# An encoder layer on one core: PSUM laid out by stage with two shared doubles, the output projection in two blocks of 384, and w_in loads moved in the queue

## The chip, the cores and the metric

The kernel runs on one core of a Trainium2 chip. The metric is the device time of one execution in microseconds (us); times are given as the median of several runs. The engines are TensorE (PE, matmuls; PEld are its weight loads), VectorE (DVE), ScalarE (ACT), GpSimd (POOL) and SyncE (SP, which here only issues DMAs). Each has its own instruction stream and works through it in order; they wait for each other by semaphores. PE writes its products into PSUM, a memory of eight banks of 2 KB per partition, from which DVE and ACT read. Everything else works in SBUF.

## What is computed

One layer of an encoder over 512 prompt tokens and 256 sample tokens (two sequences with the same weights), model width 1024, all in fp32:

```
x = layer_norm(ALPHA * x + 0.5 * swiglu(x, ffn1_up, ffn1_down), ln1_g, ln1_b)
u = x @ w_in
u_a, u_b, gate_a, gate_b = split(u)
h_a = rwkv7_branch(u_a, ...) @ w_branch_a        # bidirectional state scan, 8 heads of 64
h_b = retention_branch(u_b, pos) @ w_branch_b    # 4 heads of 128
mix = (sigmoid(gate_a) * h_a + sigmoid(gate_b) * h_b) @ w_out
x = layer_norm(ALPHA * x + mix, ln2_g, ln2_b)
x = layer_norm(ALPHA * x + 0.5 * swiglu(x, ffn2_up, ffn2_down), ln3_g, ln3_b)
```

## The kernel before, in words

Activations lie feature-major: eight tiles of 128 features by 768 tokens (T), of which columns 0 to 511 are the prompt and 512 to 767 the sample (SEGS). fp32 products are made from three fp32r products: `split` (L189 to L191) writes a high part (a cast on ACT) and a low part (a subtraction on DVE), and `mm3` (L202 ff.) sums high by high, high by low and low by high; all these matmuls carry L201. `wtile` (L152 to L163) loads a weight tile on SP's queue (`wr`, L160) and splits it (`wh` L161, `wl` L162).

The stages follow each other: the first feed-forward network (0 to about 530 us, products of 128x384 by a scheme of Strassen's kind, on the halves of the 768 tokens); its layer norm and two lead projections; the preparation (about 576 to 1027 us), in which `prep` and `invert` make the operands of the RWKV scan while `ret_seq` (L640 ff.) computes retention as a filler; the scan (1016 to 1316 us), whose PE order is written by hand (`manual_schedule`), with the gate projections as filler; the merge (`w_b`, `w_a`, then `w_out` with the second layer norm); the second feed-forward network (1507 to 2013 us) and the third layer norm. Outside the hand-written part a scheduler orders each engine's instructions, and it places an instruction by when buffers are expected to come free; so a change of buffers changes the order.

**PSUM.** A double is a tile of 768 fp32 columns in two banks (tag `mm`); a single bank has tag `pc`. `mmps` (L92 to L96) hands out doubles in turn: one lies in a pool `pre` that lives from the start to the scan, the others in the stage's own pool (`psum`, L81). A double can be handed out again when its last reader is done. Before, the first network, the preparation and retention share one pool: `pre` and one more double, and four single banks. The scan has `pre`, four single banks and two for `w`. Merge and second network share a pool of two doubles and four single banks. `small` (L101 to L108, matmuls at L105) uses two single banks, one for each segment. Score tiles of retention (L670, read by the multiplication L673) take a double; its outputs (L679) a single bank; the variance of its norm a double, read last by `osq` (L236).

**Queue around the first network's end.** The last down-projection weights (`in_f1d`, issued at L325) and the first tiles of `w_in` (L160, and L610 for retention's values) are both issued on SP. The `w_in` tiles take buffers of a pool that opens only when the network's are given up, so the issue waits for those.

**Merge.** `merge` loads the retention output (`yb`, tile `t`, L1131) head by head into two buffers (TQ), splits each into `yh` and `yl` (`pair`, L1134 ff.), and multiplies by `w_b` with the gate (`gated`). `finish` closes the last two feature blocks of the RWKV branch (`fin`). `out` (L1151 ff.) multiplies by `w_out` in blocks of columns, BLK[2], and `layer_norm` follows block by block; KEEPO says how many of the eight weight tiles are kept in SBUF from block to block (`reuse`, L177). MPE and VPE say for each block whether sums over features go through PE (1) or are first added up on DVE (0).

Of the kernel before, what the change touches and what calls it, by code (L numbers as in the profile page):

```python
# [8 lines left out]
F32 = mybir.dt.float32  # L9
# [6 lines left out]
PSUM = bass.MemoryType.PSUM  # L16
DRAM = bass.MemoryType.DRAM

P = 128
# [3 lines left out]
T = TP + TS  # L23
SEGS = ((0, TP), (TP, T))
HALVES = ((0, 256), (256, 512), (512, T))
BLK = {1: SEGS, 2: HALVES, 3: SEGS}
FF = 2816
NF = FF // P
W = 512
# [18 lines left out]
FILLS = (2, 1, 2, 1, 1, 1)  # L48
TAIL = ()
EARLY = ('A03', 'B10', 'B11', 'B12', 'B13', 'D03')  # L50
MPE = {1: (0, 1), 2: (0, 0, 0), 3: (0, 1)}
VPE = {1: (1, 1), 2: (0, 0, 1), 3: (1, 1)}
KEEP = 4
CHUNKS = (6, 6, 5, 5)
TH = T // 2
LEAD = 4
RAWS = 10
AHEAD = 9
KEEPO = 1
TQ = 2  # L60
FIN = {0: 1, 1: 1, 2: 1, 3: 1}

# [6 lines left out]
class Builder:  # L69
# [8 lines left out]
        self.n += 1  # L78
        return f"{s}{self.n}"

    def psum(self, ctx, pre=None, **bufs):  # L81
        self.pre, self.turn = pre, 2
        self.pb = bufs
        self.ps = ctx.enter_context(self.tc.tile_pool(name=self.nm("ps"), bufs=1, space=PSUM))

# [4 lines left out]
        return (pool or self.bp).tile([P, T], F32, tag=tag, name=self.nm(s))  # L90

    def mmps(self):  # L92
        self.turn += 1
        if self.pre and self.turn % (self.pb["mm"] + 1) == 0:
            return self.pre.tile([P, T], F32, tag="mm", name=self.nm("mm"))
        return self.ps.tile([P, T], F32, tag="mm", name=self.nm("mm"), bufs=self.pb["mm"])  # L96

    def bank(self, tag="pc"):
        return self.ps.tile([P, 512], F32, tag=tag, name=self.nm(tag), bufs=self.pb[tag])
# [49 lines left out]
    def vcol(self, i):  # L149
        return self.vec[:, i:i + 1]  # L150

    def wtile(self, src, dims, keep=None):  # L152
        nc = self.nc
        n = dims[0] * dims[1]
        self.tiles += keep is None
        raw = self.wp.tile([P, self.wn], F32, tag="wr", name=self.nm("wr"))[:, :n]
        pool, w = (keep, n) if keep else (self.wp, self.wn)
        hi = pool.tile([P, w], F32R, tag="wh", name=self.nm("wh"))[:, :n]
        lo = pool.tile([P, w], F32R, tag="wl", name=self.nm("wl"))[:, :n]
        nc.sync.dma_start(raw.rearrange("p (a b) -> p a b", b=dims[1]), src)  # L160
        nc.scalar.copy(hi, raw)  # L161
        nc.vector.tensor_tensor(out=lo, in0=raw, in1=hi.bitcast(F32), op=ALU.subtract)  # L162
        return tuple(t.rearrange("p (a b) -> p a b", b=dims[1]) for t in (hi, lo))  # L163

    def wparts(self, src, dims, parts):
        n = dims[0] * dims[1]
        raw = self.wp.tile([P, self.wn], F32, tag="wr", name=self.nm("wr"))[:, :n]
        hi = self.wp.tile([P, self.wn], F32R, tag="wh", name=self.nm("wh"))[:, :n]
        lo = self.wp.tile([P, self.wn], F32R, tag="wl", name=self.nm("wl"))[:, :n]
        self.nc.sync.dma_start(raw.rearrange("p (a b) -> p a b", b=dims[1]), src)  # L170
        yield tuple(t.rearrange("p (a b) -> p a b", b=dims[1]) for t in (hi, lo))
        m = n // parts
        for q in range(parts):
            self.split(*(t[:, q * m:q * m + m] for t in (raw, hi, lo)))
            yield
# [127 lines left out]
    def ffn(self, ctx, z, xs, idx, up, down, after, lead, first, then=None):  # L303
# [16 lines left out]
        def raw(src):  # L320
            out = []
            for a in range(0, src.shape[1], m):
                part = src[:, a:min(a + m, src.shape[1])]
                t = fw.tile([P, m * P], F32, tag="wr", name=self.nm("wr"), bufs=RAWS)[:, :part.shape[1] * P]
                nc.sync.dma_start(t.rearrange("p (a b) -> p a b", b=P), part)  # L325
                out.append(t)
            return out

# [268 lines left out]
    def ret_values(self, hp):  # L597
        nc, I, rp = self.nc, self.I, self.rp
        vh = rp.tile([P, 6, 256], F32R, tag="vh", name=self.nm("vh"))
        vl = rp.tile([P, 6, 256], F32R, tag="vl", name=self.nm("vl"))  # L600
        pv = []
        ws = []
        for kh in range(2):
            i = 22 + 2 * hp
            src = I["w_in"][i:i + 2, :, 4 * kh:4 * kh + 4].rearrange("w p k c -> p w k c")
            raw = self.wp.tile([P, 2, 4, P], F32, tag="wr", name=self.nm("wr"))
            wh = self.wp.tile([P, 2, 4, P], F32R, tag="wh", name=self.nm("wh"))
            wl = self.wp.tile([P, 2, 4, P], F32R, tag="wl", name=self.nm("wl"))
            for w in range(2):
                nc.sync.dma_start(raw[:, w], src[:, w])  # L610
            self.split(raw, wh, wl)
            ws.append((wh, wl))
        for tt in range(6):
            if tt % 3 == 0:
                pv.append(self.mmps())
            dst = pv[tt // 3][:, (tt % 3) * 256:(tt % 3) * 256 + 256]
            ts = slice(tt * P, tt * P + P)
            for k in range(KT):
                xh, xl = self.xs[k]
                wh, wl = ws[k // 4]  # L620
                for q, (x, w) in enumerate(((xh, wh), (xh, wl), (xl, wh))):
                    nc.tensor.matmul(dst, x[:, ts], w[:, :, k % 4], start=(k == 0 and q == 0),  # L622
                                     stop=(k == KT - 1 and q == 2))
            if tt % 3 < 2:
                continue
            g = tt // 3
            v = self.b3("v", self.rb)
            nc.scalar.copy(v, pv[g])
            mu = rp.tile([P, 6, 1], F32, tag="mu", name=self.nm("mu"))
            v3 = v.rearrange("p (a e) -> p a e", e=P)  # L630
            nc.vector.tensor_reduce(out=mu, in_=v3, op=ALU.add, axis=AX.X)
            nc.vector.tensor_scalar(mu, mu, 1.0 / P, None, ALU.mult)
            nc.vector.tensor_tensor(out=v3, in0=v3, in1=mu.to_broadcast([P, 6, P]), op=ALU.subtract)
            sl = slice(3 * g, 3 * g + 3)
            self.split(v.rearrange("p (a e) -> p a e", e=256), vh[:, sl], vl[:, sl])
        self.rv = (vh, vl)
        yield
# [232 lines left out]
                yield  # L870

    def segbanks(self):
        ps = self.pre.tile([P, T], F32, tag="mm", name=self.nm("mm"))
        return {(a, b): ps[:, a:b] for a, b in SEGS}

    def scan(self, gates, gd, gp, gt):
# [240 lines left out]
    def merge(self, zp, tp, yb, gd):  # L1117
        nc, I = self.nc, self.I
        with ExitStack() as ctx:
            tq = self.pool(ctx, "tq", TQ)  # L1120
            kp = self.pool(ctx, "kp", KEEPO)
            mp = self.pool(ctx, "mp", 8, "right")
            cy = ctx.enter_context(ExitStack())
            yq = self.pool(cy, "yq", 4)
# [57 lines left out]
                    self.split(m, h[:, a:b], l[:, a:b])  # L1182
                nc.gpsimd.dma_start(z[n], self.x1d[:, n])
            cy.close()
            kept = {}
            self.xs = [self.xpair() for _ in range(KT)]
            for i, seg in enumerate(BLK[2]):
                self.layer_norm(tp, z, 2, self.xs, seg, out(i), halves=True)
# [2 lines left out]
    def build(self, stages=9):  # L1191
# [5 lines left out]
        with ExitStack() as cx:  # L1197
            self.xp = self.pool(cx, "xp", 8)
            ca = cx.enter_context(ExitStack())
            cz = cx.enter_context(ExitStack())  # L1200
            cm = cx.enter_context(ExitStack())
            pre = ca.enter_context(self.tc.tile_pool(name="pre", bufs=1, space=PSUM))
            with ExitStack() as cw:
                self.psum(cw, pre, mm=1, pc=4)
                with ExitStack() as ctx:
                    self.first(ctx)
                self.weights(cm, D)
                cg = ca.enter_context(ExitStack())
                gt = self.pool(cg, "gt", 1, "right")
                with ExitStack() as ctx:  # L1210
                    self.ip = self.pool(ctx, "ip", 1, "right")
                    self.pp = self.pool(ctx, "pp", 1)
                    self.ret_pools(ctx)
                    seq = self.ret_seq(yb)
                    self.prep(lambda i=None: [next(seq, 0) is None for _ in range(1 if i is None else FILLS[i])][-1])
            with ExitStack() as ctx:
                gp = self.pool(ctx, "gp", 1, "right")
                self.gq = self.pool(ctx, "gq", 3)
                self.sp = [self.pool(ctx, "sp", NG // 2) for _ in range(2)]
                self.psum(ctx, pre, pc=4, w=2)  # L1220
                self.S = {}
                with self.tc.manual_schedule(engines={mybir.EngineType.PE}):
                    self.scan([*self.early, *range(AG, KT)], gd, gp, gt)
            ca.close()
            zp = self.pool(cz, "zp", 8, "right")
            self.psum(cx, mm=2, pc=4)
            with ExitStack() as ctx:
                lp = self.pool(ctx, "lp", 1, "right"), ("ln", "acc"), (4, 2)
                z = self.merge(zp, lp, yb, gd)
            cm.close()  # L1230
            for k in range(KT):
                self.dump("x2", z[k], lambda d: d[:, k])
            self.ffn(cx, z, self.xs, 3, I["f2u"], I["f2d"],
                     lambda seg, mean, lp: self.layer_norm(lp, z, 3, None, seg, mean, O["y"]),
                     LEAD, lambda load, ext, tmp: self.forms(z, self.xs, ext, tmp))
# [109 lines left out]
```

## Time and profile before

| what | value |
|---|---|
| time, median of 3 runs | 2044.17 us (2041.85 to 2051.94) |
| the profiled execution | 2045.81 us, span 2044.0 us |
| mean granted clock of TensorE | 0.965 |
| DMA | 202.62 MB, mean 99 GB/s |

The span is the time between the first and the last record of the profile. In rows of groups and chains stand the start, the length in us, the engine, the tile, the line and the count. A row of waits names who waited, for whom, the total, how often, and the longest. "SPq" and "ACTq" are the engines' own instruction queues, mostly issues of DMAs.

### The profile page before, as it was taken

The page shows a single profiled execution, that of the slowest core. Times are in us where ns is not written, and L with a number is a line of the kernel's source. Part 1 is how long each engine was busy: PE and PEld are TensorE (multiplying, and loading weights), DVE is VectorE, ACT ScalarE, POOL GpSimd, SP SyncE. Part 2 cuts the span into 40 slices and gives each one's busy share as a digit, 9 for nine tenths or more (in the row PEclk, how much of TensorE's full clock was granted, in tenths as well). Part 3 has the DMA queues.
Part 4 walks back from the last instruction along what each step waited for, and adds up shares of the span by engine and source line. Part 5 has one row for each costly group of instructions (what it writes and reads, how often), then busy time and mean ns, then how long its engine had stood idle before and what let it go on. Part 6 is the DMA issues. An engine that isn't in the chain of part 4 may idle for free.

```text
span 2044.0 us, 33681 instructions
## 1 busy us (share of the span) xinstructions
PE 1899.9 (93%) x13294; PEld 1696.7 (83%) x13294; DVE 1274.9 (62%) x2265; ACT 827.5 (40%) x1560; POOL 187.2 (9%) x290
## 2 busy tenths in 40 slices
PE   7999999998989889998799989799889999999997
PEld 7999989997777768777688767579879999899985
DVE  8846747565637584857435555377888467475665
ACT  6323323233545353634245555243663224233325
POOL 0000000000000445254420000000000000000000
PEclk9999999998899999999999989999989999999998
DMA  5222121223222333332364441546322221212221
GB/s 196 81 70 73 57 84 59 70 65 98 76 92 96 125 110 106 113 121 102 112 202 113 125 128 62 167 145 212 110 97 85 70 73 58 83 60 64 71 70 64
DMA packets 141598, 202.62 MB, mean 99 GB/s; under 512 B 55680, under 2 KB 73728, under 8 KB 141440
## 3 DMA queue, kind: packets, MB, share of 16 engines
q1 hardware_dynamic: 123904, 178.44, 27.5%
q0 software_dynamic: 3424, 14.94, 2.2%
q10 hardware_dynamic: 14112, 7.08, 1.2%
q8 instruction: 105, 1.72, 0.3%
q14 instruction: 53, 0.43, 0.1%
HBM read 158.74 MB, written 41.68 MB: 98 GB/s over the span
## 4 chain that ended last, share of the span: by engine, by line
PE 80%; DVE 9%; ACT 6%; DMA 3%; issue 2%; ACTq 0%; SPq 0%; DVEq 0%; POOLq 0%
PE mm L201 39%; PE pc L201 29%; PE mm L622 2%; PE pc L246 2%; PE pc L105 1%; PE pc L1038 1%; PE w L974 1%; ACT z L275 1%; DVE wl L162 1%; PE w L985 1%; PE pc L1086 1%; PE w L979 1%; DMA t<-ybd 1%; DVE u L402 1%; DVE z L274 1%
## 5 line engine op out<-in xcount | busy, mean ns | idle before, releaser
L201 PE MATMUL pc<-xh,ph 128*128 128x384 f32 x704 | 243.5, 346 | 20.8 <-ACT u L359 9.2
L201 PE MATMUL pc<-xl,ph 128*128 128x384 f32 x704 | 239.3, 340 | 0.1
L190 ACT CAST ph<-wr 128x512 fp32r<-128x512 f32 (+1 forms) x232 | 131.1, 567 | 220.4 <-PE mm L201 137.4
L201 PE MATMUL mm<-xh,wh 128*128 128x256 f32 (+1 forms) x640 | 181.3, 366 | 27.6 <-DVE s L673 6.1
L402 DVE TENSOR_TENSOR u<-u,pc 128x384 f32<-128x384 f32 x220 | 121.5, 552 | 88.8 <-PE pc L201 85.2
L201 PE MATMUL pc<-eh,ph 128*128 128x384 f32 x528 | 176.4, 334 | 0.0
L201 PE MATMUL pc<-el,ph 128*128 128x384 f32 x528 | 176.4, 334 | 0.0
L201 PE MATMUL mm<-xl,wh 128*128 128x512 f32 (+1 forms) x640 | 173.7, 354 | 0.0
L162 DVE TENSOR_TENSOR wl<-wr,wh 128x1024 fp32r<-128x1024 f32 (+1 forms) x76 | 83.7, 1101 | 138.0 <-PE mm L201 82.4
L201 PEld LDWEIGHTS pc<-xh,ph 128*128 128x128 f32 x704 | 134.8, 192 | 29.8 <-ACT u L359 10.3
L191 DVE TENSOR_TENSOR pl<-wr,ph 128x512 fp32r<-128x512 f32 (+1 forms) x232 | 141.5, 621 | 25.6 <-ACT ph L190 19.9
L201 PE MATMUL pc<-xh,pl 128*128 128x384 f32 x704 | 153.0, 338 | 0.8 <-DVE pl L191 0.8
L191 DVE TENSOR_TENSOR pl<-sa,ph 128x512 fp32r<-128x512 f32 x176 | 120.9, 687 | 45.6 <-ACT ph L190 45.6
L201 PEld LDWEIGHTS mm<-xh,wh 128*128 128x128 f32 x640 | 105.6, 202 | 51.5 <-issue 18.4
L201 PE MATMUL mm<-hl,ph 128*128 128x512 f32 (+1 forms) x544 | 138.8, 336 | 0.0
L201 PE MATMUL mm<-hh,ph 128*128 128x512 f32 (+1 forms) x544 | 138.8, 336 | 0.0
L201 PEld LDWEIGHTS pc<-xl,ph 128*128 128x128 f32 x704 | 134.9, 192 | 0.7 <-DVE xl L191 0.5
L161 ACT CAST wh<-wr 128x1024 fp32r<-128x1024 f32 (+1 forms) x76 | 71.2, 936 | 157.3 <-PE mm L201 130.4
L201 PEld LDWEIGHTS pc<-xh,pl 128*128 128x128 f32 x704 | 126.5, 191 | 1.3 <-DVE pl L191 1.2
L190 ACT CAST ph<-sa 128x512 fp32r<-128x512 f32 x176 | 105.4, 617 | 54.8 <-DVE sa L351 26.3
L201 PE MATMUL mm<-xh,wl 128*128 128x512 f32 (+1 forms) x640 | 125.4, 346 | 0.0
L201 PEld LDWEIGHTS mm<-xl,wh 128*128 128x128 f32 x640 | 104.3, 200 | 15.9
(313 smaller groups left out, 3967.2 us busy)
## 6 DMA issues: line engine op xcount, KB each, us to landing
wr<-in_f1u SPq DMA_DIRECT2D x96, 256.0 KB, 3.2
wr<-in_f2u SPq DMA_DIRECT2D x96, 256.0 KB, 3.1
wr<-in_w_in SPq DMA_DIRECT2D x30, 512.0 KB, 3.5
wr<-in_f1d SPq DMA_DIRECT2D x37, 256.0 KB, 2.7
wr<-in_f2d SPq DMA_DIRECT2D x37, 256.0 KB, 2.7
wr<-in_w_out SPq DMA_DIRECT2D x18, 512.0 KB, 3.5
wr<-in_w_in SPq DMA_DIRECT2D x32, 256.0 KB, 3.5
dd<-ar SPq DMA_DIRECT2D x8, 768.0 KB, 3.3
```

Source lines behind the costliest of these rows:

```text
L105: self.nc.tensor.matmul(ps, w, x[:, a:b], start=True, stop=True)
L161: nc.scalar.copy(hi, raw)
L162: nc.vector.tensor_tensor(out=lo, in0=raw, in1=hi.bitcast(F32), op=ALU.subtract)
L190: self.nc.scalar.copy(hi, src)
L191: self.nc.vector.tensor_tensor(out=lo, in0=src, in1=hi.bitcast(F32), op=ALU.subtract)
L201: self.latest = self.nc.tensor.matmul(o, w, x[:, a:b], start=start and i == 0, stop=stop and i == len(terms) - 1, skip_group_check=more).ins
L246: self.summed = nc.tensor.matmul(st["ps"], self.ones, src, start=k == 0, stop=k == KT - 1).ins
L274: nc.vector.scalar_tensor_tensor(out=zk, in0=zk, scalar=-0.5, in1=rs, op0=ALU.mult, op1=ALU.mult)
L275: nc.scalar.activation(zk, zk, AF.Identity, bias=self.vcol(g0 + 8 + k), scale=self.vcol(g0 + k))
L402: add = lambda o, a, b: nc.vector.tensor_tensor(out=o, in0=a, in1=b, op=ALU.add)
L622: nc.tensor.matmul(dst, x[:, ts], w[:, :, k % 4], start=(k == 0 and q == 0), stop=(k == KT - 1 and q == 2))
L974: nc.tensor.matmul(pb[64 * h:64 * h + 64, C * j:C * j + C], sc[:, c % 4, h, 1], vu[:, c % 4, h], start=True, stop=True)
```

## The change

PSUM: `pre` becomes a tuple of shared doubles. The first network now gets two shared doubles and four single banks; the preparation and retention get these two, one more of their own (three in turn), and two single banks. The scan has the first of the two, four single banks and two for `w`, as before. The merge gets two shared doubles and one of its own and two single banks; the second network the two and four single banks.

Output projection and second normalisation: two blocks, columns 0 to 383 and 384 to 767, where there were three of 256; sums of the first block's squares on DVE and of the second's on PE. Four weight tiles of `w_out` are kept where one was, so there are 10 loads and splits in place of 18, and the pool for them is opened behind the one of the retention output's split.

Queue: `fetch` makes the first six DMA issues of `w_in` follow the last weight load of the first network.

```diff
-BLK = {1: SEGS, 2: HALVES, 3: SEGS}
+BLK = {1: SEGS, 2: ((0, T // 2), (T // 2, T)), 3: SEGS}
...
-MPE = {1: (0, 1), 2: (0, 0, 0), 3: (0, 1)}
-VPE = {1: (1, 1), 2: (0, 0, 1), 3: (1, 1)}
+MPE = {1: (0, 1), 2: (0, 0), 3: (0, 1)}
+VPE = {1: (1, 1), 2: (0, 1), 3: (1, 1)}
...
-KEEPO = 1
+GATED = 6
+KEEPO = 4
...
-    def psum(self, ctx, pre=None, **bufs):
-        self.pre, self.turn = pre, 2
+    def psum(self, ctx, pre=(), **bufs):
+        self.pre, self.turn = pre, -1
...
     def mmps(self):
-        self.turn += 1
-        if self.pre and self.turn % (self.pb["mm"] + 1) == 0:
-            return self.pre.tile([P, T], F32, tag="mm", name=self.nm("mm"))
-        return self.ps.tile([P, T], F32, tag="mm", name=self.nm("mm"), bufs=self.pb["mm"])
+        n = self.pb.get("mm", 0)
+        self.turn = (self.turn + 1) % (len(self.pre) + n)
+        if self.turn < len(self.pre):
+            return self.pre[self.turn].tile([P, T], F32, tag="mm", name=self.nm("mm"))
+        return self.ps.tile([P, T], F32, tag="mm", name=self.nm("mm"), bufs=n)
...
+    def fetch(self, dst, src):
+        self.gated += 1
+        with self.tc.issue_after(self.gate) if self.gated <= GATED else ExitStack():
+            self.nc.sync.dma_start(dst, src)
...
-                nc.sync.dma_start(t.rearrange("p (a b) -> p a b", b=P), part)
+                self.gate = nc.sync.dma_start(t.rearrange("p (a b) -> p a b", b=P), part).ins
+                self.gated = 0
...
-            kp = self.pool(ctx, "kp", KEEPO)
...
             cy.close()
-            kept = {}
+            kept, kp = {}, self.pool(ctx, "kp", KEEPO)
...
-            pre = ca.enter_context(self.tc.tile_pool(name="pre", bufs=1, space=PSUM))
+            double = lambda c: c.enter_context(self.tc.tile_pool(name=self.nm("pre"), bufs=1, space=PSUM))
+            pre = double(ca),
             with ExitStack() as cw:
-                self.psum(cw, pre, mm=1, pc=4)
+                two = *pre, double(cw)
                 with ExitStack() as ctx:
+                    self.psum(ctx, two, pc=4)
                     self.first(ctx)
+                self.psum(cw, two, mm=1, pc=2)
...
-            self.psum(cx, mm=2, pc=4)
+            two = [double(cx) for _ in range(2)]
             with ExitStack() as ctx:
+                self.psum(ctx, two, mm=1, pc=2)
...
             cm.close()
+            self.psum(cx, two, pc=4)
```

`wtile`, the weight splitter of the first network and `ret_values` call `fetch` where they called `nc.sync.dma_start`; the lines of the changed file lie seven or eight further on. Where instructions move:

SP's queue at the first network's end; `wr` are weight tiles, `in_f1d` the down projection, `in_w_in` the projection into the branches. Before:

```order
L325 DMA wr_4579<-in_f1d 128x512
L325 DMA wr_4581<-in_f1d 128x128
L160 DMA wr_5462<-in_w_in 128x1024
L610 DMA wr_5523<-in_w_in 128x512 x2
L610 DMA wr_5530<-in_w_in 128x512 x2
L325 DMA wr_4707<-in_f1d 128x512
```

Now, from the last of the 22 remaining `in_f1d` loads on:

```order
L332 DMA wr_5143<-in_f1d 128x512
L332 DMA wr_5145<-in_f1d 128x128
L332 DMA wr_5252<-in_w_in 128x512
L332 DMA wr_5254<-in_w_in 128x512
L332 DMA wr_5264<-in_w_in 128x512
L332 DMA wr_5266<-in_w_in 128x512
L157 DMA wr_5469<-in_w_in 128x1024
L157 DMA wr_5530<-in_w_in 128x512 x2
L157 DMA wr_5537<-in_w_in 128x512 x2
L157 DMA wr_5709<-in_w_in 128x1024
```

All six issues of the projection tiles now stand behind the four of the lead projections (L332).

PE in the preparation, at the first score tiles of retention (`mm` from `qh`), with the small products of the RWKV branch (`pc` from `lt`) and the marks of what waits. Before:

```order
L105 MATMUL pc_6059<-lt,lora_5458 128x512
L105 MATMUL pc_6061<-lt,lora_5458 128x256
L105 MATMUL pc_6067<-lt,lora_5458 128x512 [waits Activation_49]
L105 MATMUL pc_6069<-lt,lora_5458 128x256 [waits Activation_49]
L670 MATMUL mm_5997<-qh_5699,qh_5846 128x512 [waits DMAHW3_49,DMAHW2_49,DMAHW6_49,DMAHW1_49,DMAHW7_49,DMAHW0_49,Activation_49]
L670 MATMUL mm_5997<-ql_5700,qh_5846 128x512
L670 MATMUL mm_5997<-qh_5699,ql_5847 128x512 [waits DVE_49]
L799 MATMUL mm_6018<-ar_6005,kb_6006 64x64 [waits DVE_49,PE_49]
```

Now:

```order
L678 MATMUL mm_6004<-qh_5706,qh_5853 128x512 [waits DMAHW2_49,DMAHW3_49,DMAHW1_49,DMAHW6_49,DMAHW0_49,DMAHW7_49,PE_49,Activation_49]
L678 MATMUL mm_6004<-ql_5707,qh_5853 128x512
L678 MATMUL mm_6004<-qh_5706,ql_5854 128x512 [waits DVE_49]
L107 MATMUL pc_6066<-lt,lora_5465 128x512 [waits Activation_49]
L107 MATMUL pc_6068<-lt,lora_5465 128x256 [waits Activation_49]
L807 MATMUL mm_6025<-ar_6012,kb_6013 64x64 [waits DVE_49]
L807 MATMUL mm_6025<-ar_6012,kb_6013 64x64 x23
L107 MATMUL pc_6074<-lt,lora_5465 128x512 [waits Activation_49]
L107 MATMUL pc_6076<-lt,lora_5465 128x256 [waits Activation_49]
```

The first pair of small products now waits for a reader on ACT where it waited for none, and the two pairs stand apart, with other products between them.

SP's queue in the scan's last periods; `t` are the buffers of the retention output (`ybd`) and of the gates (`gd`), the `in_w_in` tiles weights of the last gates. Before:

```order
L1131 DMA t_13007<-ybd 128x768
L1131 DMA t_13017<-ybd 128x768
L160 DMA wr_12810<-in_w_in 128x512
L160 DMA wr_12867<-in_w_in 128x512
L160 DMA wr_13062<-in_w_b 128x2x512
L160 DMA wr_13153<-in_w_b 128x2x512
L160 DMA wr_13233<-in_w_b 128x2x512
L160 DMA wr_13297<-in_w_b 128x2x512
L1166 DMA fin_13047<-dd_5401 128x768
L1166 DMA fin_13048<-dd_5401 128x768
L1131 DMA t_13027<-ybd 128x768
L1131 DMA t_13037<-ybd 128x768
```

Now:

```order
L1138 DMA t_13018<-ybd 128x768
L1138 DMA t_13028<-ybd 128x768
L157 DMA wr_12818<-in_w_in 128x512
L1138 DMA t_13038<-ybd 128x768
L1138 DMA t_13048<-ybd 128x768
L1138 DMA t_13080<-gd 128x768
L1138 DMA t_13125<-gd 128x768
L157 DMA wr_12875<-in_w_in 128x512
L157 DMA wr_13073<-in_w_b 128x2x512
```

The second two loads of the retention output, and the first two of the gates, went ahead of the last gate weight and of all of `w_b`. On ACT and DVE the eight casts and eight subtractions of the split moved with them, from behind the last gate's activation to between the scan's steps three gates earlier.

More of the change, by code (lines that the diff above doesn't have):

```diff
@@ L159, in wtile @@
         lo = pool.tile([P, w], F32R, tag="wl", name=self.nm("wl"))[:, :n]
-        nc.sync.dma_start(raw.rearrange("p (a b) -> p a b", b=dims[1]), src)
+        self.fetch(raw.rearrange("p (a b) -> p a b", b=dims[1]), src)
         nc.scalar.copy(hi, raw)
@@ L169, in wparts @@
         lo = self.wp.tile([P, self.wn], F32R, tag="wl", name=self.nm("wl"))[:, :n]
-        self.nc.sync.dma_start(raw.rearrange("p (a b) -> p a b", b=dims[1]), src)
+        self.fetch(raw.rearrange("p (a b) -> p a b", b=dims[1]), src)
         yield tuple(t.rearrange("p (a b) -> p a b", b=dims[1]) for t in (hi, lo))
@@ L609, in ret_values @@
             for w in range(2):
-                nc.sync.dma_start(raw[:, w], src[:, w])
+                self.fetch(raw[:, w], src[:, w])
             self.split(raw, wh, wl)
@@ L872, in segbanks @@
     def segbanks(self):
-        ps = self.pre.tile([P, T], F32, tag="mm", name=self.nm("mm"))
+        ps = self.pre[0].tile([P, T], F32, tag="mm", name=self.nm("mm"))
         return {(a, b): ps[:, a:b] for a, b in SEGS}
```

## The prediction

> **What bounds the kernel now.** I read the page's busy times first, then the table of windows by stage, then TensorE's (PE's) waits and the chain of waits in the stages where PE is not full. The page says who the bound is:
>
> ```profile
> span 2044.0 us, 33681 instructions
> PE 1899.9 (93%) x13294; PEld 1696.7 (83%) x13294; DVE 1274.9 (62%) x2265; ACT 827.5 (40%) x1560; POOL 187.2 (9%) x290
> ```
>
> PE is idle for 2044.0 − 1899.9 = 144.1 us. The change removes no PE work (below), so all it can win lies in that idle time and in matmuls that run slowly behind it. The windows (length, then busy us of PE, PEld, DVE, ACT, POOL, then granted clock, DMA share, GB/s) say where:
>
> ```profile
> 600.00:700.00 100.00, 94.84 (x618) 79.11 (x618) 63.33 (x83) 44.21 (x58) 9.19 (x19) 0.98 0.29 98
> 700.00:800.00 100.00, 90.50 (x528) 72.25 (x526) 66.87 (x87) 42.96 (x59) 48.40 (x72) 0.95 0.38 126
> 800.00:910.00 110.00, 102.04 (x647) 84.58 (x646) 74.17 (x95) 51.07 (x66) 47.23 (x72) 0.97 0.33 111
> 910.00:1027.00 117.00, 98.77 (x567) 79.69 (x568) 68.56 (x86) 42.96 (x60) 60.00 (x84) 0.93 0.34 111
> 1314.90:1369.90 55.00, 40.46 (x200) 32.67 (x201) 32.93 (x49) 19.84 (x28) 4.23 (x8) 0.88 0.56 191
> 1403.70:1475.70 72.00, 69.96 (x586) 69.04 (x584) 56.60 (x120) 34.36 (x58) 1.06 (x2) 1.00 0.38 122
> 1475.70:1507.20 31.50, 15.90 (x67) 14.34 (x67) 22.88 (x56) 22.68 (x52) 0.00 (x0) 0.79 0.48 158
> ```
>
> The feed-forward networks' bodies are left as they are. Idle are the preparation (600 to 1027: 94.84 + 90.50 + 102.04 + 98.77 = 386.2 of 427, so 40.9 idle), the way from the scan to the merge (14.5 of 55), and the way into the second network (15.6 of 31.5). The output projection itself is full: 70.0 of 72.
>
> **The change part by part.** I go in order of time.
>
> *The w_in loads behind the last raw loads.* The chain of waits at the first network's end, and at the same place of the second, which has no w_in to load:
>
> ```profile
> 483.16 4.18 PE pc L201 x24
> ...
> 487.36 4.11 DMA wr<-in_w_in
> ...
> 491.55 1.05 ACT wh L161
> ...
> 492.63 1.24 DVE wl L162
> ...
> 499.42 26.39 PE mm L201 x120
> ...
> 1966.96 4.18 PE pc L201 x24
> ...
> 1976.47 25.22 PE mm L201 x120
> ```
>
> ```profile
> SPq L160 <- PE pc L201: 35.8, 1, 35.8
> ```
>
> SyncE stood 35.8 us in front of one w_in load, whose buffer was held until the last product's matmul (487.34), and the last down-projection weights (f1d) were queued behind it. From there to the next block PE has 499.42 − 487.34 = 12.1 us; the second network needs 1976.47 − 1971.14 = 5.3. With w_in moved behind the raw loads I expect the 5.3, so 6.8, and the block of 120 matmuls at 25.22 in place of 26.39, so 1.2 more: **−8**. What the moved loads do later: their casts (1.05 on ACT) and subtractions (1.24 on VectorE, DVE) now stand among those of the first normalisation. Two of each, if nothing covers them, cost 2 × 2.3 = 4.6; PE has matmuls of the lead projections there, so I take nothing. On SyncE the six issues stand behind the lead projections' four loads and ahead of the stores of x1d; nothing on PE reads them before the lead projections are done. Bounds: −3 to −10.
>
> *Three doubles and two single banks in the preparation.* PE's waits, 575 to 1030 (total, times, longest):
>
> ```profile
> PE mm L670 <- DVE s L673: 10.4, 6, 3.1
> PE mm L201 <- DVE s L673: 6.1, 4, 2.9
> PE mm L201 <- DVE t L699: 5.1, 1, 5.1
> PE mm L201 <- ACT s L833: 5.0, 1, 5.0
> PE mm L201 <- DVE osq L236: 4.9, 1, 4.9
> PE mm L201 <- DVE k L699: 3.8, 2, 2.4
> ```
>
> All but the osq row are waits until a reader frees a double: 10.4 + 6.1 + 5.1 + 5.0 + 3.8 = 30.4. The osq row stays, since the scan's first gate tile still lies on the banks of the last variance. Neither DVE (63.33 + 66.87 + 74.17 + 68.56 = 272.9 of 427, 64%) nor ACT (181.2, 42%) is full there, so the waits are queues at a moment and not a rate; a third double lets PE go one tile further in that time. What one tile is worth:
>
> ```profile
> 667.19 1.18 PE mm L670 x3
> 682.14 8.50 PE mm L201 x48
> 946.67 14.48 PE mm L201 x69
> ```
>
> A projection tile (48 matmuls, 8.50) covers any single wait of the list; a score tile (3 matmuls, 1.18) doesn't, and of the 10.4 I leave half, of the other 20.0 a fifth, for two waits that follow on each other: 30.4 − 5.2 − 4.0 gives 21 won. Against it stands the pool of single banks, from four to two: a pair of small products (L105) takes both, so the next pair waits until ACT or DVE has read them. In PE's order 55 of these rows now carry a wait, where 29 did: 26 more. A reader takes:
>
> ```profile
> L768 ACT ACTIVATE e<-pc,half x16: 466/578/690, 620.9 to 933.0; 128x512 f32<-128x512 f32 x8, 128x256 f32<-128x256 f32 x8
> ```
>
> 26 × 0.578 = 15 if each waits for a whole reader, nothing if all are read in time; most pairs now have 20 or more projection matmuls between them, at 8.50 / 48 = 0.177 each 3.5 us of cover, so I take 4, nearer to nothing. Net **−17**. Bounds: a third of 30.4 won with 15 lost, +5, to all won, −30.
>
> The last row above has a further lesson: 69 matmuls at 0.177 would be 12.2 and took 14.48, behind a wait of 5.0. Each long wait so costs some 2.3 more. I leave that out of the sum, as a reserve on the deep side. [...]
>
> *From the scan into the merge.* The chain:
>
> ```profile
> 1318.04 11.87 DMA t<-ybd
> ...
> 1366.94 0.69 DVE z L1148
> 1367.63 1.80 DVE yl L191 x3
> 1369.91 5.68 PE mm L201 x24
> ```
>
> The second two retention heads (ybd) are only fetched once the scan is over; in the order of the changed kernel their loads and their split stand in the scan's last periods. PE's work from 1314.9 to 1369.9 is eight tiles of 24 matmuls (8 × 4.25 = 34.0, half of 8.50 each) and the small products of the finish. It is busy for 40.46; of the 6.5 over the eight tiles I put half, 3, to slow matmuls behind the waits (the granted clock is 0.88). With the 14.5 idle, 17.5 is the most to be won. What is late next is the finish of the last two feature blocks (z and yl, 0.69 + 1.80 and their gaps, 3.0 before w_a starts): it stays. Third, the split itself now stands in the scan, whose ACT and DVE are in order:
>
> ```profile
> 1273.77 1.04 SPq L1131 DMA_DIRECT2D t<-ybd  x2
> ```
>
> ```profile
> 1278.11 0.62 ACT L161 CAST wh<-wr 128x512 fp32r<-128x512 f32 x1 [1.46 <-PE w L963]
> 1316.34 1.75 ACT L190 CAST yh<-t 128x512 fp32r<-128x512 f32 x4 [0.54 <-DVE wl L162]
> ```
>
> ```profile
> t<-ybd SPq DMA_DIRECT2D x4, 384.0 KB, 8.5
> ```
>
> Eight casts are 2 × 1.75 = 3.5 on an ACT that has pauses of one to three us between its steps there; I take 0.6. 17.5 − 3.0 − 0.6: **−14**. Bounds: −5 (the finish's own loads hold it) to −17.
>
> *w_out in two blocks.* Runs of full-rate matmuls with 384 columns (in the first network) and with 256 (here):
>
> ```profile
> 171.56 87.90 PE pc L201 x504
> ...
> 1431.42 7.83 PE mm L201 x67
> ```
>
> A matmul of 384 takes 87.90 / 504 = 0.174, one of 256 takes 0.117: by the column. So 24 × 8 × 3 × 0.117 = 67.4 becomes 24 × 8 × 2 × 0.174 = 66.8, which is nothing. The four kept weights go into memory that the retention output's split has long left, so nothing waits for that. Eight loads of 512 KB, eight casts and eight subtractions less lie beside a full PE: 2.0 idle is all there is. **−2**, bounds −4 to +2.
>
> *The way into the second network.* Its first half of tokens (0 to 383) needed two normalised blocks of the three, now one, finished while PE still multiplies the other:
>
> ```profile
> 1475.70 3.15 DMA wr<-in_f2u
> ...
> 1485.54 5.23 PE pc L201 x17
> ```
>
> ```profile
> PE pc L255 <- DVE acc L253: 3.4, 1, 3.4
> ```
>
> The weights still land 3.15 after the last matmul of w_out and are cast after that, so the first products can start near 1480 and not at 1485.5: 5. DVE comes to the last block without the middle one's remains, which I put at the acc wait, 3.4. The last block is half as wide again; I charge 1.4 for it. **−7**, bounds +3 (the wider block governs) to −11.
>
> **The sum.** −8 − 17 − 14 − 2 − 7 = −48, against the profiled execution's 2045.81 (its span 2044.0 and 1.8 around it; the median, 2044.17, is 0.1% lower, which I neglect): 1997.8, so **1998**.
>
> **The rivals.** *The third double wins nothing*: the readers are paced by VectorE's chain of elementwise work, and PE meets the same reader one tile later. For it: the score tiles, six of the waits, are only 1.18 us each. Against: DVE is at 64%. Then the preparation costs its 4: 2045.8 − 8 + 4 − 14 − 2 − 7 = 2019. [...]
>
> *The split blocks the scan's tail*: ybd's loads land 8.5 us after issue in the median; the second pair can only be asked for when the first is split, and ACT and DVE stand in order before the scan's next state update. The first pair, issued at 1273.8, would land near 1282.3 where ACT comes at 1278.7; the second, one split later, some 7 us behind ACT; with the gate weights queued behind them about 15 is lost, and the merge's 14 is gone: 2012.
>
> *The two single banks cost more than all gains* (the slower side): 26 more waits, each as long as the queue in front of the reader. The gains without that term are 48 + 4 = 52, so at 52 / 26 = 2.0 us each the change is nothing; from 2.4 us on it is slower by more than 0.5%. At 3.1, the longest of the score waits, it is 81: 2045.8 − 52 + 81 = 2075. For it: score waits average 10.4 / 6 = 1.7. Against: the new order puts projection matmuls between most pairs.
>
> **How the numbers follow.** Forecast 0.71; the third double wins nothing 0.12; the blocked scan 0.08; bank waits of 1.6 to 2.4 us (no change) 0.05; above that 0.04. About 0.5%, 10 us, is what a measurement of this kernel can tell from no change. So faster 0.71 + 0.12 + 0.08 = 0.91, same 0.05, slower 0.04. The deep end takes all bounds but a little, 2045.8 − 10 − 30 − 17 − 4 − 11 = 1974, drawn in to 1976, since not all fall deep at once; the upper end goes over both faster rivals (2019) with 11 us of room for weak terms, 2030. That leaves out the last two cases and some tail.
>
> **What would show it.** Right: no w_in load ahead of f1d in SyncE's queue and some 5 us before the block of 120; preparation's idle near 20 in place of 41, with the s L673 rows (there L681) at most half; no ybd wait behind the last gate; first products of the second network within 6 us of the last w_out matmul. Wrong: rows of PE pc L107 or L687 (the small products and the retention outputs in the changed file) waiting on ACT or DVE with over 10 us in all; ACT waiting for DMA t<-ybd inside the scan; the same 15 us idle before the second network.

## The result, and the profile after

The changed kernel takes 1984.35 us (median of 4 runs, 1980.87 to 1990.57), the kernel before 2043.01 (4 runs): a ratio of 0.971, with a 95% interval of 0.967 to 0.975. The forecast was 1998 with a range of 1976 to 2030. The profiled execution has a span of 1981.0 us, 63.0 less than before. The first part of its page, on the engines' busy time:

```profile
span 1981.0 us, 33145 instructions
PE 1886.8 (95%) x13098; PEld 1685.0 (85%) x13098; DVE 1259.4 (64%) x2208; ACT 807.0 (41%) x1521; POOL 190.3 (10%) x290
```

PE's idle time went from 144.1 to 94.2 us, and PE is also busy for 13.1 us less. Most of those 13.1 are the same matmuls, run faster (below). Where the 63 went can be read from marks that both programs have: the end of the first network's last product, the end of its block of 120 matmuls, the moment at which PE's wait for `t` ends, the start of the scan's first gate tile, the last gate's activation, the first load of the second network's weights (issued when the last `w_out` matmul is done), and the end of the second network's last product.

| from one mark to the next | before, us | after, us | difference | forecast |
|---|---|---|---|---|
| first network's end | 38.5 | 30.5 | −8.0 | −8 |
| first normalisation | 58.7 | 58.7 | 0 | 0 |
| preparation | 437.1 | 400.6 | −36.5 | −17 |
| scan | 293.3 | 292.6 | −0.7 | 0 |
| merge and output projection | 160.8 | 144.6 | −16.2 | −14 − 2 |
| way into the second network, and its body | 495.4 | 493.4 | −2.1 | −7 |
| end | 72.9 | 73.1 | +0.3 | 0 |

The marks of the scan and behind it, from the chain of waits before:

```profile
1021.63 9.29 PE mm L201 x40
...
1314.93 0.88 ACT gt L868 x2
```

From the chain after, then from its timelines of ACT and SP:

```profile
977.35 9.82 PE mm L208 x40
...
1903.70 4.18 PE pc L208 x24
```

```profile
1269.92 0.87 ACT L876 ACTIVATE gt<-mm 128x512 f32<-128x512 f32 x2 [0.98 <-PE mm L208]
```

```profile
1414.53 13.70 SPq L332 DMA_DIRECT2D wr<-in_f2u  x15
```

At the first network's end the chain of waits of the changed kernel has no load in it any more:

```profile
483.33 4.18 PE pc L208 x24
...
488.19 0.97 DVE u L427
...
492.86 25.17 PE mm L208 x120
```

From 487.51 to 492.86 PE has 5.35 us, where it had 12.1: the same 5.3 that the second network always had. In the preparation, PE's longest waits (total, times, longest) are these:

```profile
PE mm L208 <- DVE t L707: 5.1, 1, 5.1
PE mm L208 <- DVE osq L243: 4.6, 1, 4.6
PE pc L107 <- DVE v L707: 3.4, 4, 2.1
PE mm L220 <- DVE s L681: 2.3, 2, 1.2
PE mm L208 <- DVE s L681: 1.4, 1, 1.4
PE pc L687 <- DVE sl L198: 1.3, 1, 1.3
```

Of the score tiles' 10.4 + 6.1 the projections still wait 1.4. The rows for the gate (`s` L833, 5.0) and for `k` (3.8) are gone. The wait for `osq` stays, as said, and so does the one for `t`, which I had counted among those that a third double could take away. The windows from the end of the wait for `t` to the end of the second gate's activation hold practically the same work in both, before first:

```profile
584.54:1043.48 458.94, 416.58 (x2512) 340.34 (x2512) 276.51 (x354) 194.46 (x261) 173.08 (x261) 0.95 0.35 117
```

```profile
576.76:999.72 422.96, 405.98 (x2500) 332.19 (x2500) 274.72 (x354) 188.47 (x257) 176.19 (x260) 0.99 0.38 126
```

The stretch is 36.0 shorter. PE's idle time in it falls from 42.4 to 17.0, by 25.4, and its busy time by 10.6; the granted clock rises from 0.95 to 0.99. The 12 matmuls fewer are products for retention's values (L622 before, L630 now): the changed kernel does 12 of them, 1.43 us of work, ahead of the wait for `t`. So some 9 of the 10.6 are the same matmuls, run faster.

In the scan's last part, ACT's timeline shows the split of the retention output where it now stands, between the scan's steps, and no load of `ybd` behind the last gate's activation at 1269.92:

```profile
1232.36 1.75 ACT L197 CAST yh<-t 128x512 fp32r<-128x512 f32 x4
...
1238.43 0.92 ACT L197 CAST yh<-t 128x512 fp32r<-128x512 f32 x2 [2.18 <-DMA t<-ybd]
...
1240.55 0.93 ACT L197 CAST yh<-t 128x512 fp32r<-128x512 f32 x2 [0.67 <-DMA t<-ybd]
```

ACT waits for the second pair of loads, but 2.18 + 0.67 us in place of the 15 of the rival that feared a blocked scan. On the way into the second network, the same 31.5 us behind the last `w_out` matmul are these:

```profile
1414.53:1446.03 31.50, 20.04 (x78) 14.93 (x79) 23.98 (x48) 21.53 (x43) 0.00 (x0) 0.89 0.45 149
```

PE is idle for 11.5 us of them, where it was idle for 15.6.

### The profile page after: what moved, and what is told of

It is laid out like the page before. It is cut to its first block, busy times and chain, and to the rows that moved or that the text cites. A ratio compares the mean times of both kernels' runs of the same rounds, so it can differ in the third digit from the quotient of the medians.

```text
span 1981.0 us, 33145 instructions
## 1 busy us (share of the span) xinstructions
PE 1886.8 (95%) x13098; PEld 1685.0 (85%) x13098; DVE 1259.4 (64%) x2208; ACT 807.0 (41%) x1521; POOL 190.3 (10%) x290
## 4 chain that ended last, share of the span: by engine, by line
PE 82%; DVE 9%; ACT 4%; DMA 3%; issue 2%; SPq 0%; ACTq 0%; POOL 0%; DVEq 0%; POOLq 0%
PE mm L208 39%; PE pc L208 30%; PE pc L253 2%; PE mm L630 2%; PE pc L107 2%; PE pc L1046 1%; DMA t<-gd 1%; PE w L982 1%; PE pc L1094 1%; PE pc L687 1%; DVE z L281 1%; PE w L993 1%; DVE u L410 1%; PE w L987 1%; PE pc L1055 1%
## 5 line engine op out<-in xcount | busy, mean ns | idle before, releaser
L208 PE MATMUL mm<-xh,wh 128*128 128x512 f32 (+1 forms) x640 | 177.2, 356 | 15.0 <-DVE t L707 5.1
L198 DVE TENSOR_TENSOR pl<-wr,ph 128x512 fp32r<-128x512 f32 (+1 forms) x232 | 141.6, 623 | 20.6 <-ACT ph L197 20.6
L169 DVE TENSOR_TENSOR wl<-wr,wh 128x1024 fp32r<-128x1024 f32 (+1 forms) x68 | 74.8, 1100 | 92.7 <-PE mm L208 47.2
L168 ACT CAST wh<-wr 128x1024 fp32r<-128x1024 f32 (+1 forms) x68 | 62.7, 922 | 139.0 <-PE mm L208 112.7
```

The costliest lines, as they stand in the source:

```text
L198: self.nc.vector.tensor_tensor(out=lo, in0=src, in1=hi.bitcast(F32), op=ALU.subtract)
L208: self.latest = self.nc.tensor.matmul(o, w, x[:, a:b], start=start and i == 0, stop=stop and i == len(terms) - 1, skip_group_check=more).ins
```

## The experiments

Each is measured beside the kernel before on the same chip. Where two versions are compared by a part of their time, the part is read from their profiles between the marks above. A difference to the changed kernel's whole time compares medians from separate measurements, beside which the kernel before had medians of 2043.01 to 2046.71.

### The preparation: third double, and two single banks

```diff
-                self.psum(cw, two, mm=1, pc=2)
+                self.psum(cw, two, pc=4)
```

> The changed kernel with two doubles and four single banks in the preparation, as before. Theory (the third double wins the preparation's 36 us, 25 of them waits and 11 slower matmuls behind waits): from the first projection behind the wait on t to the scan's first gate tile it takes 437 us again and not 401, PE's idle time there is about 46 and its busy time about 11 more; the whole is about 2020. Rival (the gain comes from the earlier weights and another order of instructions): within 8 us of the changed kernel.

Measured: 2014.46 us (ratio 0.986, 0.983 to 0.989), 30 more than the changed kernel. The window from the end of the wait for `t` to the second gate, and the largest of PE's waits:

```profile
573.06:1028.24 455.18, 417.56 (x2512) 342.06 (x2512) 277.07 (x354) 194.28 (x261) 166.78 (x260) 0.95 0.34 113
```

```profile
PE mm L678 <- DVE s L681: 10.6, 6, 3.1
PE mm L208 <- DVE s L681: 6.2, 5, 2.9
PE mm L208 <- DVE t L707: 5.1, 1, 5.1
PE mm L208 <- ACT s L841: 5.1, 1, 5.1
PE mm L208 <- DVE k L707: 3.7, 2, 2.3
```

These are the rows of before to within 0.2. The stretch is 455.2, 32.2 longer than the changed kernel's, of which 20.6 is idle time (37.6 against 17.0) and 11.6 is busy time (417.6 against 406.0, the 12 moved matmuls included), at a clock of 0.95 again. So the division of PSUM wins both parts, and the rival (within 8 us) is refuted. It wins 32.2 of the 36.0; the other 3.8, by which this version is shorter than the kernel before, were not traced to anything. This run swaps the third double for two single banks; the next one tells the two apart.

```diff
-                self.psum(cw, two, mm=1, pc=2)
+                self.psum(cw, two, pc=2)
```

> The changed kernel with two doubles and two single banks in the preparation (two banks of PSUM lie idle). Theory (the smaller pool of single banks only costs, a few us): slower than with two doubles and four banks by 3 to 8 us, about 2025. Rival (two single banks make the schedule put products apart, and that is part of the gain): faster than with two doubles and four banks by 8 us or more.

Measured: 2011.03 us (0.984, 0.980 to 0.987), 3 less than with four banks. The intervals overlap, though on this one chip none of the four runs here (2009.46 to 2013.66) is as long as the shortest with four banks (2014.02). The stretch:

```profile
576.46:1024.46 448.00, 414.76 (x2512) 338.90 (x2512) 278.14 (x354) 189.26 (x257) 172.53 (x260) 0.97 0.35 115
```

It is 7.2 shorter than with four banks. So my theory that the smaller pool costs falls, and the rival, 8 us or more of the total, isn't shown either: two single banks cost nothing here; whether they win a little, because the schedule sets the products further apart, was not shown. Against this version the changed kernel has the third double and nothing else, and that is what the third double is worth by itself: 25.0 us of the stretch, 16.3 of idle time (33.2 against 17.0) and 8.8 of busy time (414.8 against 406.0, the 12 moved matmuls included), and 26.7 of the whole. It is no accident of one execution: from the end of the wait for `t` to the start of the second gate's activation the changed kernel and the five versions below that share its preparation take 422.0 to 423.4, the two versions here 454.3 and 447.1, the kernel before 458.1 and, with its pool moved, 463.3.

### The merge: place of the split's tiles, third double

```diff
             tq = self.pool(ctx, "tq", TQ)
+            kp = self.pool(ctx, "kp", KEEPO)
...
-            kept, kp = {}, self.pool(ctx, "kp", KEEPO)
+            kept = {}
...
-KEEPO = 4
+KEEPO = 1
```

> The changed kernel with the pool for kept w_out weights opened ahead of the retention output's pool as before, and one kept tile, so that the split's tiles lie where they lay before. Theory (the merge's gain comes from where those tiles lie: lower memory is free before the scan ends, so the split moves into the scan): PE waits some 11 us for yh behind the last gate again, and the whole is 10 to 18 us longer, about 1998. Rival (the third double in the merge wins it): at most 3 us longer.

Measured: 1994.90 us (0.977, 0.973 to 0.980), 10.6 more than the changed kernel. The two intervals touch (the changed kernel's ends at 0.975), but the four runs here (1992.24 to 2002.80) all lie above the changed kernel's (1980.87 to 1990.57). PE's longest waits from the last gate on:

```profile
PE mm L208 <- ACT yh L197: 11.2, 2, 9.1
PE pc L262 <- DVE acc L260: 2.9, 1, 2.9
```

The wait for `yh` is back at 11.2, with all three doubles in place; from the last gate to the second network's first load it takes 154.9, and not 144.6. This run also keeps one weight tile in place of four; the reverse, on the kernel before, moves the pool and nothing else:

```diff
-            kp = self.pool(ctx, "kp", KEEPO)
...
-            kept = {}
+            kept, kp = {}, self.pool(ctx, "kp", KEEPO)
```

> The kernel before, with the one edit that the pool for kept w_out weights is opened behind the retention output's pool (one kept tile as before, all else as before). Theory (this place alone brings the split into the scan and wins the merge's time): no wait of PE for yh behind the last gate over 2 us, and 8 to 16 us less than the kernel before, about 2032. Rival (it needs the rest of the change, the third double above all): within 4 us of the kernel before.

Measured: 2032.68 us against 2044.14 on the same chip (0.994, 0.992 to 0.996), 11.5 less. The timeline of ACT shows the split ahead of the last three gates, and from the last gate to the first load of the second network's weights it takes 144.8 (1320.27 to 1465.07), where the kernel before needs 160.8:

```profile
1282.87 1.75 ACT L190 CAST yh<-t 128x512 fp32r<-128x512 f32 x4
1289.23 0.92 ACT L190 CAST yh<-t 128x512 fp32r<-128x512 f32 x2 [2.53 <-DMA t<-ybd]
1290.90 0.92 ACT L190 CAST yh<-t 128x512 fp32r<-128x512 f32 x2 [0.22 <-DMA t<-ybd]
...
1320.27 0.87 ACT L868 ACTIVATE gt<-mm 128x512 f32<-128x512 f32 x2 [0.98 <-PE mm L201]
```

PE has no wait for `yh` there any more. One line of code, which names neither PSUM nor a queue, so wins the merge's whole part, 16.0 in the profiles and 11.5 by the medians of the whole. With the pool `kp` in front, the split's tiles lie 8 KB per partition higher, and their upper end then lies on the scan's `ar` tiles. In the instructions of the kernel before, the first cast waits for the store of the last of these; the trace of before has that store at the very end of the scan:

```profile
1313.98 0.37 ACTq L1005 DMA_DIRECT2D dd<-ar  x1
...
1316.34 1.75 ACT L190 CAST yh<-t 128x512 fp32r<-128x512 f32 x4 [0.54 <-DVE wl L162]
```

With `kp` behind, the tiles end where `ar` begins, and the split waits for its loads only. The third double of the merge by itself:

```diff
-                self.psum(ctx, two, mm=1, pc=2)
+                self.psum(ctx, two, pc=4)
                 lp = self.pool(ctx, "lp", 1, "right"), ("ln", "acc"), (4, 2)
```

> The changed kernel with two doubles and four single banks in the merge; the early split of the retention output stays. Theory (the place of the split's tiles wins most of the merge's 16 us, the third double some of it): from the last gate's activation to the first load of the second network's weights 2 to 6 us more than the changed kernel's 144, the whole at most 8 us longer, no long wait for yh. Rival (the third double wins it): 10 us or more longer, with PE waiting for readers of doubles.

Measured: 1981.45 us (0.969, 0.967 to 0.970), no more than the changed kernel, and 141.3 from the last gate to the second network's load, 3 less than the changed kernel's 144.6. PE waits for readers of doubles a little longer (2.7 against 2.6 in all), and that is all:

```profile
PE mm L208 <- DVE z L1155: 2.7, 4, 1.0
```

The 2 to 6 us that I gave to the third double in the merge are not there.

### The queue at the first network's end

```diff
-GATED = 6
+GATED = 0
```

> The changed kernel with the six w_in issues no longer held behind the last raw load. Theory (the queue order wins 8 us at the first network's end): the block of 120 matmuls starts again 12 us after the last product, not 5.3, and the whole is 6 to 9 us longer than the changed kernel (about 1992 against 1984). Rival (the time was won in the layer norm behind it, whose weights now come at another time): the block of 120 starts as in the changed kernel and the whole moves by under 2 us.

Measured: 1994.81 us (0.976, 0.973 to 0.979), 10.5 more than the changed kernel. The chain:

```profile
482.52 4.18 PE pc L208 x24
...
486.71 4.17 DMA wr<-in_w_in
...
494.14 3.87 DMA wr<-in_f1d
...
498.76 27.02 PE mm L208 x120
```

The block starts 12.1 after the last product, and ends 39.1 after it in place of 30.5: 8.6 of the 10.5. From there to the end of the wait for `t` it takes 57.3, against 58.7 in the changed kernel; the kernel before, which has this order, shows both (58.7, and 57.3 in the version with its pool moved), so nothing is shown to be won or lost in the normalisation behind, and the rival falls. The profiled executions differ by 15.9, more than the medians; most of what is left of that lies in the scan (280.7 from the second gate to the last, against 271.1), to which the last section comes back.

### The output projection's blocks, and the second normalisation

```diff
-BLK = {1: SEGS, 2: ((0, T // 2), (T // 2, T)), 3: SEGS}
+BLK = {1: SEGS, 2: HALVES, 3: SEGS}
...
-MPE = {1: (0, 1), 2: (0, 0), 3: (0, 1)}
-VPE = {1: (1, 1), 2: (0, 1), 3: (1, 1)}
+MPE = {1: (0, 1), 2: (0, 0, 0), 3: (0, 1)}
+VPE = {1: (1, 1), 2: (0, 0, 1), 3: (1, 1)}
```

> The changed kernel with output projection and second normalisation in three blocks of 256 again (four kept weights, so 12 loads). Theory (two blocks win next to nothing: PE was full in the output projection, and the way into the second network got only 2 us shorter): within 4 us of the changed kernel. Rival (the two blocks won the merge's time): 8 us or more longer.

Measured: 1984.77 us (0.970, 0.967 to 0.973), the changed kernel's time. From the last gate to the load 146.5 (144.6 in the changed kernel), from there to the last product of the second network 491.7 (493.4): +1.9 and −1.7. Two blocks win nothing that can be measured.

```diff
-VPE = {1: (1, 1), 2: (0, 1), 3: (1, 1)}
+VPE = {1: (1, 1), 2: (0, 0), 3: (1, 1)}
```

> The changed kernel with the second block's sum of squares added up on VectorE and not by 16 matmuls. Theory (the 16 matmuls, 8 us of them, stand in PE's order ahead of the second network's first products, which is why these began 17 us behind the last matmul of the output projection and not 4): the first products begin at least 5 us earlier, and the whole is 2 to 6 us shorter, about 1980. Rival (the normalisation of the second block, on VectorE and ScalarE, is what the network waits for): the first products earlier, but the wait behind them longer by as much; within 2 us or up to 4 us longer, since seven additions join VectorE's work.

Measured: 1987.84 us (0.972, 0.970 to 0.973), not shorter. The timeline of PE behind the last matmul of `w_out` (at 1414.5), in the changed kernel, then in this one (last matmul at 1412.6):

```profile
1415.73 0.91 PE L262 MATMUL pc<-acc,ones 128*128 128x384 f32 x2 [1.24 <-DVE acc L260]
1421.27 8.09 PE L253 MATMUL pc<-ln,ones 128*128 128x384 f32 x16 [4.62 <-ACT ln L275]
1431.88 0.41 PE L208 MATMUL pc<-xh,ph 128*128 128x384 f32 x1 [2.52 <-issue]
```

```profile
1413.84 0.91 PE L262 MATMUL pc<-acc,ones 128*128 128x384 f32 x2 [1.24 <-DVE acc L260]
1429.14 1.65 PE L262 MATMUL pc<-acc,ones 128*128 128x384 f32 x2 [14.39 <-DVE acc L260]
1433.31 0.66 PE L208 MATMUL pc<-xh,ph 128*128 128x384 f32 x1 [2.52 <-issue]
```

The theory misses. The 16 matmuls are gone, but the sum of squares from VectorE is one matmul that stands at the same place of PE's order, and it comes 14.4 later. The first products begin 20.7 behind the last matmul and not 17.4. The experiment so shows that the wait is for the variance, by whichever engine it is summed. That the first products themselves did not need the variance is in the timeline of DVE in the changed kernel, where the low parts of their operands are written, each behind its high part:

```profile
1411.88 2.43 DVE L198 TENSOR_TENSOR xl<-z,xh 128x384 fp32r<-128x384 f32 x5
...
1418.09 0.69 DVE L198 TENSOR_TENSOR pl<-wr,ph 128x512 fp32r<-128x512 f32 x1 [2.41 <-ACT ph L197]
```

The inputs are there at 1414.3 and the first weight tile at 1418.8, 13 us before the first product at 1431.88. What the whole would win if these products stood ahead of the variance no run here tried.

### The wait in front of the scan

```diff
                 self.psum(cw, two, mm=1, pc=2)
+                self.turn = 0
                 self.weights(cm, D)
```

> The changed kernel with the three doubles of the preparation handed out one place further on, so that the last variance of retention does not lie on the banks of the scan's first gate tile. Theory (PE's wait for osq ahead of the scan, 4.6 us, is a wait for these banks alone): the wait goes, the first gate tile is multiplied while the norm is worked out, and the whole is 4 to 8 us shorter, about 1978. Rival (the scan's first products need operands that come no earlier): the gate tile earlier, the scan's first own products at the same time, within 2 us.

Measured: 1979.66 us (0.967, 0.965 to 0.969). PE's wait for `osq` is gone, and the scan's first gate activation is at 982.15, where the changed kernel has it at 989.13; the second at 993.31 and not 998.84. But the last one in the profiled execution is at 1270.88 against 1269.92: this scan took 277.6 from the second gate to the last, the changed kernel's 271.1. The whole is 4.7 less by the medians, as forecast, but the intervals overlap.

```diff
                 self.psum(cw, two, mm=1, pc=2)
+                self.turn = 0
                 self.weights(cm, D)
...
-                self.psum(ctx, two, mm=1, pc=2)
+                self.psum(ctx, two, pc=4)
                 lp = self.pool(ctx, "lp", 1, "right"), ("ln", "acc"), (4, 2)
```

> The changed kernel with the doubles of the preparation handed out one place further on, and with two doubles and four single banks in the merge: the two single edits that looked no worse than the changed kernel. Theory (the wait for osq was worth its 4.6 us, and the third double in the merge nothing): about 1979, 3 to 8 us under the changed kernel's 1984. Rival (the scan's own length, which differs from run to run by more than that, decides): within 3 us of 1984.

Measured: 1977.63 us (0.968, 0.965 to 0.970), the lowest median of all. Its scan took 276.9. Its interval overlaps the changed kernel's (0.967 to 0.975), so it beats the kernel before, and whether it beats the changed one by the 6.7 us of the medians stays unclear.

## Why the prediction was right, and where it was off

The time lies in the range and the direction was forecast; the gain of 48 was 63 in the profile, 59 by the medians. The range held although its largest term, the preparation, was less than half of what it should have been: that miss of 19 us was in part made up by the way into the second network, which won 5 less than its term, and that part is luck. By its steps:

- *The w_in loads, −8.* Right in mechanism and size: 8.0 in the profile, 8.6 when undone. The moved casts and subtractions cost nothing that shows, since the stretch of the first normalisation is 58.7 in both.
- *Preparation, −17.* The mechanism was right and the size wrong, beyond its own bound of −30. Three things were mis-sized. I left half of the score waits and a fifth of the others standing, and nearly all but the wait for `t` went: idle time fell by 25.4, where the sum had 21. I charged 4 for the two single banks; with two doubles beside them they show no cost. And I put the slow matmuls behind the waits aside "as a reserve", with the row in hand that priced them (2.3 behind a wait of 5.0): the sum had nothing for PE's busy time, which fell by 10.6, some 9 of it faster matmuls. A wait of PE can have two prices here, the wait and a slower clock afterwards, and both belong in the sum. In the kernel before, the granted clock was 0.50 in the first 2.3 us behind the wait of 5.0 and 1.00 from 4.8 us on; behind the longest wait of a projection for a score tile (2.9) it was 0.62 in the first 2.2 us. Not every wait had the second price: behind one of 2.4 for `k`, and behind two of 1.35 for score tiles, it was 1.00 at once. Over the stretch the means agree with that: 0.95 and 0.97 with two doubles, 0.99 with three.
- *Scan to merge, −14, and two blocks, −2.* 16.2 together, right in size. The early split does it, as said. What moves the split I had not seen: it isn't the doubles but the place of the pool `kp`, and that line alone is worth 11.5 on the kernel before. The blocks show no gain.
- *Into the second network, −7.* It was 2.1. The step that failed is that the first products could start near 1480, 4 us behind the last matmul of `w_out`: they start 17.4 behind it, later than in the kernel before (9.8), because PE's order puts the variance of the second block in front of them, and that waits for squares and subtractions on ACT and VectorE. Their operands were there after 4.3 us, as I had reckoned; I costed the load and the casts, and not PE's order. Of my sign of being wrong, the same 15 us idle there, 11.5 came.
- *The rivals.* That the third double wins nothing is refuted by its removal. The blocked scan: its sign came, ACT waits for the loads of `ybd` inside the scan, but for 2.9 us, and the scan isn't longer (292.6 against 293.3). The waits for single banks: L107 and L687 come to 5.3 us in all, some 3 more than before, not 52.

## What to carry to other kernels

Where PE waits many times for a reader of its product, count the slow matmuls behind the waits with them; here one more buffer won 16 us of idle time and some 7 more of matmul time. Before crediting a gain to the buffers that a change names, look at where its tiles lie in memory: a pool opened further down let a whole step run a stage earlier, 11.5 us. A load that waits for a buffer belongs behind the loads of its queue that wait for nothing; here that was worth 8 us at one place.

## What the runs showed that was not expected

The scan does not always take as long: from the second gate's activation to the last it was 271.1 us in the changed kernel, 280.7 in the version that has the same scan and another order of loads at the first network's end, and 281.8 where the merge's pool was moved. Beside the changed kernel, the 10.7 of the last one lie in two places. Between the fourth and the fifth gate, first the changed kernel, then the other:

```profile
1077.29:1122.66 45.37, 43.61 (x730) 37.64 (x732) 23.98 (x80) 27.93 (x78) 0.54 (x1) 0.92 0.44 127
```

```profile
1076.39:1127.06 50.67, 43.10 (x730) 37.10 (x732) 24.08 (x80) 27.98 (x78) 0.54 (x1) 0.93 0.41 113
```

Here PE is idle for 5.8 us more. Between the sixth gate and the seventh PE is busy longer, 49.7 us for 656 matmuls in place of 43.5, at a clock of 0.75 and not 0.90; a stretch of that part ran with PE busy all the time at half the clock, behind one in which PE was busy for 5.5 us of ten:

```profile
1180.00:1190.00 10.00, 5.47 (x53) 4.86 (x54) 3.54 (x14) 7.35 (x18) 0.00 (x0) 0.66 0.31 107
1190.00:1200.00 10.00, 10.00 (x116) 8.46 (x114) 2.48 (x9) 3.86 (x11) 0.00 (x0) 0.50 0.01 2
```

Near the first place VectorE waits longer for a load issued by GpSimd in the finish of the first feature blocks. The rows for the scan, first the changed kernel, then the one with the pool moved, then the kernel before:

```profile
DVE finy L1105 <- DMA finz<-dd: 5.0, 2, 3.0
```

```profile
DVE finy L1105 <- DMA finz<-dd: 8.0, 2, 5.4
```

```profile
DVE finy L1097 <- DMA finz<-dd: 11.3, 2, 8.8
```

The kernel before waits longest for these loads and has a short scan (272.3), so the late load alone does not make a scan long. What does stays open. The four versions measured on one chip have 276.6 to 281.8, the four on another 272.0 to 277.6, so the chip may have a part in it. It means that in this kernel a gain of some 5 us ahead of the scan can't be read from one profile of the whole, as with the wait for `osq`.
